# A two-layer block on one core: small fp32 products regrouped, bias rows at the head, two sets of scan tables

## The chip, the cores and the metric

The kernel runs on one core of a Trainium2 chip. The metric is device time in microseconds of one execution, lower is better; the time of a kernel is the median of its runs.

## The reference, cut to what matters

Two layers over 1024 tokens of width 1024, in fp32. The change touches the first layer alone:

```python
h = rmsnorm(x, norm_mix_pre)
q, k, v, u, g_attn, g_ssm = jnp.split(h @ w_in, SPLITS, axis=-1)
y_attn = sliding_window_attention(q, k, v, sinks, rel_bias) @ w_attn_branch
z = gelu(s5_ssm(u, lam_re, lam_im, log_dt, b_re, b_im, c_re, c_im, d_skip))
z = z * sigmoid(z @ w_glu)
merged = sigmoid(g_attn) * y_attn + sigmoid(g_ssm) * (z @ w_ssm_branch)
x = x + rmsnorm(merged @ w_out, norm_mix_post)
```

The attention has 8 query heads of 64 over 2 key heads; a block of 128 queries sees its own and the previous block of keys, with a bias by bucketed distance and a sink per head. The scan has 32 groups of 16 channels, each with a complex diagonal state of 64. A feed-forward block follows, and then the second layer with three gated branches.

## The kernel before, in words

Large products are done in f16 with each operand split into a high and a low half (`split`, L134, one ACT and one DVE operation): three f16 products of 128x128 by 512 for one in fp32. Most go by Strassen's scheme: `strassen` (L267) registers a unit that runs `pair_products` (L189) for a pair of 128-column blocks, seven products of 12 matmuls into four PSUM banks, and a preparation, `prep` (L151), that loads the weights through SP into one of four `raw` buffers and makes seven pairs of halves. `linear2` (L333) is the plain form with 512 rows of weights.

Units stand in `units` in the order of the text and are emitted so, each unit's preparation two units ahead (L1484). The order of instructions on each engine isn't the text's: the framework's planner issues, by its own estimate of times, the earliest operation in the text that is ready. So products of different units are mixed on PE, and each engine then runs its list strictly in order. An operation on a piece of memory waits for all earlier ones in the text that touch the same bytes. Most memory is one array, the arena, addressed in KB by hand (`A32(kb, n)`), so two uses of the same KB order each other. PSUM has two tags of four banks, `bank` for the f16 products and `aux` for the rest.

The units that matter, in the order of the text:

- The head (L526): eight tiles of x are loaded, normalized (ACT squares, POOL power, DVE scaling), turned on PE and split.
- `first_pair` (L359) for keys and values and for half of the queries, then key copies and `sums_later` (L498), then `strassen` for the other half of the queries.
- The bias (L571): eight products spread one head's row of 384 over 128 partitions, ACT copies them, a POOL DMA stores 1.5 MB, and a second one reads it back along diagonals into `bias_t`.
- The scan's parameters (L623): some hundred small DVE operations in a chain (exponentials, sine and cosine, powers), with loads through POOL; scratch comes from `tmp` at 92 to 108 KB. They leave `Ar`, `Ai`, `Bf`, `CT`, `Fs` and others.
- Attention (L810), block by block: `attend(n)` (L760) makes logits of 8 heads into aux banks, DVE adds the bias and takes the row maximum (L773), ACT does the exponentials, DVE scales (L786) into one of two buffers `Pb` at 92 to 108 KB. `values(n - 1)` (L788) turns the probabilities four tiles at a time, ACT copies them (L802), and products of 256 columns go into 64 of the 128 partitions of a bank (L805).
- Two Strassen units for u, whose results are stored through `us` at 132 to 140 KB to DRAM, then four for the attention's gates (`gate_ahead(GA)`).
- The scan (L978): for each of four chunks `ssm_tables(uc)` makes Ft, CA and Gt on DVE, the products `pwk` (L919) of the table Kt (copied to `Wsb`, then eight POOL DMAs) and turned Gt; `ssm_scan(uc)` (L935) makes S (L942), rotates, scans and rotates back on DVE, and then the output products `py` (L967 with Kt, L969 with CA and the states) and a gelu. The arena of the scan starts at 56 KB, where the queries lie.
- Four gates for the scan's branch, four `linear2` with `w_attn_branch`, the GLU (L1006 to L1021) that reads z back, and the branch with `w_ssm_branch`.

Products between fp32 operands show as two records (two weight loads and two matmuls) in the profile, transposes as one. A product over 64 partitions, or into 64, uses half of the array: `64*128` in a row is 64 input rows by 128 output columns, `128*64` the other way.

## Time and profile before

| | us |
|---|---|
| median of 3 runs | 2021.39 |
| lowest and highest run | 2015.39, 2022.36 |
| the profiled execution | 2019.8 |
| its span | 2018.1 |
| PE busy | 1972.1 (98%) |
| DVE busy | 1535.8 (76%) |
| ACT busy | 897.6 (44%) |

The span is the profiled execution from its first to its last instruction. A matmul's length in the profile includes its tail, which overlaps the next one; what a product takes in a stream is seen from start to next start. The granted clock (PEclk) is TensorE's, as a share of full speed.

### The profile page before, as it was taken

Reading aid. Unit: us, or ns where it says so; the run is one execution under the profiler, and the core shown is the slowest. Engines: PE = TensorE matmul, PEld = TensorE weight load, DVE = VectorE, ACT = ScalarE, POOL = GpSimd, SP = SyncE. Lnnn points to the kernel's source line nnn. Section 1 sums busy time; section 2 is a strip of 40 time slices with the busy share of each in tenths; the row PEclk is TensorE's granted clock in tenths of the full one; section 3 lists DMA queues with packets and bytes.
Section 4 is the critical chain, followed back from the end, with each engine's and each line's share of the span. In section 5 each row is a group of like instructions: output and inputs, shape, how many; then the busy total and the mean of one; then the engine's idle time right before and its main releaser. Section 6 shows DMA issues by size and latency. Waiting matters only on the chain. (4 is left out here: it accounts for less than half of the span.)

```text
span 2018.1 us, 25890 instructions
## 1 busy us (share of the span) xinstructions
PE 1972.1 (98%) x9536; PEld 939.9 (47%) x9536; DVE 1535.8 (76%) x2830; ACT 897.6 (44%) x1691; POOL 93.1 (5%) x157
## 2 busy tenths in 40 slices
PE   7989999999999999999999998999999999999998
PEld 4434545554454444444445444454444444444443
DVE  7787678777758876877876767679788797889843
ACT  7326553234346634724626645435333343345411
POOL 1000010110010000000000021000000000000000
PEclk9989999899999999999999999999999999999999
DMA  5322072477422122122122422111212133332122
GB/s 178 101 89 74 32 131 70 128 230 266 151 84 73 43 63 63 42 63 63 56 67 94 140 88 80 50 46 50 64 54 72 43 89 78 77 90 80 62 78 85
DMA packets 132880, 176.01 MB, mean 87 GB/s; under 512 B 12281, under 2 KB 98549, under 8 KB 132624
## 3 DMA queue, kind: packets, MB, share of 16 engines
q1 hardware_dynamic: 124736, 160.46, 24.6%
q0 software_dynamic: 5840, 12.84, 3.7%
q8 instruction: 75, 1.23, 0.2%
q10 hardware_dynamic: 2176, 1.05, 0.2%
q14 instruction: 53, 0.43, 0.1%
HBM read 138.01 MB, written 30.93 MB: 84 GB/s over the span
## 5 line engine op out<-in xcount | busy, mean ns | idle before, releaser
L206 PE MATMUL b<-arena,whi 128*128 128x512 f16 x2044 | 776.4, 380 | 6.4 <-DVE u L235 3.0
L207 PE MATMUL b<-arena,whi 128*128 128x512 f16 x2044 | 776.8, 380 | 1.3 <-DVE arena L136 1.3
L208 PE MATMUL b<-arena,wlo 128*128 128x512 f16 x2044 | 776.4, 380 | 0.0
L135 ACT ACTIVATE whi<-raw 128x512 f16<-128x512 f32 x553 | 332.2, 620 | 517.0 <-PE b L207 246.6
L136 DVE SCALAR_TENSOR_TENSOR wlo<-raw,whi 128x512 f16<-128x512 f32 x553 | 369.7, 678 | 77.0 <-ACT whi L135 75.7
L207 PEld LDWEIGHTS <-whi 128*128 128x128 f16 x2044 | 200.2, 98 | 249.5 <-issue 16.4
L206 PEld LDWEIGHTS <-whi 128*128 128x128 f16 x2044 | 200.4, 98 | 242.5 <-issue 6.5
L208 PEld LDWEIGHTS <-wlo 128*128 128x128 f16 x2044 | 200.3, 98 | 242.3 <-issue 6.1
L251 DVE SCALAR_TENSOR_TENSOR c<-b,u 128x512 f32<-128x512 f32 x204 | 139.5, 685 | 54.5 <-PE b L208 54.3
L413 PEld LDWEIGHTS <-arena 128*128 128x128 f16 x1152 | 112.7, 98 | 133.3
L413 PE MATMUL po<-arena 128*128 128x512 f16 x384 | 84.0, 379 | 0.0
L413 PE MATMUL pf<-arena 128*128 128x512 f16 x384 | 84.0, 379 | 0.0
L413 PE MATMUL pw<-arena 128*128 128x512 f16 x384 | 83.0, 379 | 0.0
L352 PE MATMUL pl<-arena,whi 128*128 128x512 f16 x320 | 82.3, 379 | 0.1
L229 DVE SCALAR_TENSOR_TENSOR u<-b,p 128x512 f32<-128x512 f32 x79 | 54.2, 686 | 35.5 <-PE b L208 33.2
L235 DVE SCALAR_TENSOR_TENSOR u<-b,u 128x512 f32<-128x512 f32 x79 | 54.2, 686 | 33.3 <-PE b L208 33.1
L381 PE MATMUL pq<-arena,whi 128*128 128x512 f16 (+1 forms) x288 | 78.3, 357 | 0.0
L224 ACT ACTIVATE p<-b 128x512 f32<-128x512 f32 x79 | 46.2, 585 | 46.9 <-PE b L208 46.8
L432 ACT ACTIVATE hn<-xr 128x512 f32<-128x512 f32 x32 | 19.9, 623 | 90.5 <-issue 40.1
L841 ACT ACTIVATE c<-c 128x512 f32<-128x512 f32 x60 | 37.6, 628 | 41.7 <-DVE c L251 41.7
L135 ACT ACTIVATE arena<-c 128x512 f16<-128x512 f32 x67 | 41.9, 626 | 24.0 <-DVE c L1370 20.6
L1097 ACT ACTIVATE c<-c 128x512 f32<-128x512 f32 x45 | 28.3, 630 | 53.1 <-DVE c L251 53.0
(325 smaller groups left out, 2157.1 us busy)
## 6 DMA issues: line engine op xcount, KB each, us to landing
raw<-in_w_in_dram SPq DMA_DIRECT2D x86, 512.0 KB, 4.0
raw<-in_w_ff_in_dram SPq DMA_DIRECT2D x32, 512.0 KB, 4.5
raw<-in_w_ff_out_dram SPq DMA_DIRECT2D x32, 512.0 KB, 3.7
fetch<-gdr SPq DMA_DIRECT2D x32, 256.0 KB, 4.8
xr<-xdr SPq DMA_DIRECT2D x32, 256.0 KB, 3.5
gdr<-c SPq DMA_DIRECT2D x24, 256.0 KB, 2.0
arena<-in_x_dram SPq DMA_DIRECT2D x8, 512.0 KB, 10.1
raw<-in_w_out_dram SPq DMA_DIRECT2D x8, 512.0 KB, 5.1
```

Source lines behind the costliest of these rows:

```text
L135: ACT(hi, src, AF.Copy, scale=scale)
L136: STT(lo, src, scale, hi, ALU.mult, ALU.subtract)
L206: MM(b[:, 0:n], whi[:, k], act[0][:, i, k, sl], start=(first and k == 0), stop=False, skip_group_check=not first)
L207: MM(b[:, 0:n], whi[:, k], act[1][:, i, k, sl], start=False, stop=False, skip_group_check=not first)
L208: MM(b[:, 0:n], wlo[:, k], act[0][:, i, k, sl], start=False, stop=(k == nk - 1), skip_group_check=not first)
L224: ACT(v["p1"], o1, AF.Copy, scale=scale)
L229: STT(v["u2"], o2, scale, v["p1"], ALU.mult, ALU.add)
L235: STT(v["u3"], o, scale, v["u2"], ALU.mult, ALU.add)
L251: STT(d, vw(o), scale, vw(v[u]), ALU.mult, ALU.add)
L352: MM(bs[s], w[:, k], a[:, k, s * H:(s + 1) * H], start=(k == 0 and w is hi and a is act[0]), stop=(k == 3 and w is lo))
L381: MM(o, w[:, k % 4], a, start=(k == 0 and w is hi and a is ahi), stop=(k == 7 and w is lo))
L413: MM(bs[s], part(a), w[:, s * H:(s + 1) * H], start=(k == 0 and a is ahi and w is whi), stop=(k == nk - 1 and a is alo))
```

## The change

- **Bias.** One product makes all eight rows on 8 partitions, at the head, right after the second tile of x is issued. A small DRAM buffer takes them, and a DMA spreads them to 128 copies in DRAM; both are on SP. The read along diagonals moves from POOL to SP and stands right after the first two projections.
- **Values.** The transposes are grouped by key half and key head, and one bank takes all products of a block, 512 columns each, into the lower 64 partitions for key head 0 and the upper for 1, in turn. This permutes the rows of the branch's input, so `linear2` can load its weights in that order (`by_kv`), by two DMAs of 64 partitions.
- **Parameters' scratch** moves from 92 to 108 KB to 131 to 136 KB, and some of it to 142 to 144 KB.
- **pwk** goes to four column groups (partitions 0, 32, 64 and 96), and is copied by eight small ACT copies a chunk.
- **py** is a function of its own, `ssm_out`: first all products with Kt, then those with CA, the two row halves in turn.
- **Two sets** of Kt, Ft and CA; the tables of chunk uc + 1 stand in the text between scan and output products of chunk uc. Vt gets a place of its own.

```diff
@@ -330,12 +330,20 @@
         return add
-    def linear2(W, c0, act, cb, scale, early=None):
+    def linear2(W, c0, act, cb, scale, early=None, by_kv=False):
         ws = []
         def prepare():
-            raw = load_k(W, lambda w: w.rearrange("(k p) n -> p k n", p=P), c0)
+            if by_kv:
+                raw = pw.tile([P, 4, 256], F32, tag="raw", name=nm("raw"), bufs=NR)
+                for a in range(2):
+                    nc.sync.dma_start(out=raw[64 * a:64 * a + 64],
+                                      in_=W[256 * a:256 * a + 256].rearrange("(k p) n -> p k n", p=64)[:, :, c0:c0 + 256])
+            else:
+                raw = load_k(W, lambda w: w.rearrange("(k p) n -> p k n", p=P), c0)
             for c in range(2):
                 ws.append(hl_tile())
...
@@ -522,6 +530,29 @@
     a21_1 = Flat(144)
     g_pre = A32(140, D)
     K32 = [A32(92 + 8 * q, 4 * H).rearrange("p (k t) -> p k t", k=4) for q in range(4)]
+    bias_t = A32(84, 8 * 256).rearrange("p (h s) -> p h s", h=8)
+    sink = small([P, 8], "sink")
+    bdr = pdr.tile([P, 8 * 384], F32, tag="bdr", name="bdr")
+    def bias_rows():
+        relb = small([33, 8], "relb")
+        nc.vector.memset(relb, 1.0)
+        nc.gpsimd.dma_start(out=relb[0:32, :], in_=I["rel_bias"])
+        hot, row = A32(88, 384)[0:33, :], A32(89.5, 384)[0:8, :]
+        nc.gpsimd.dma_start(out=hot, in_=I["onehot"])
+        pb = aux("pbias")
+        MM(pb[0:8, 0:384], relb, hot, start=True, stop=True)
+        nc.scalar.copy(row, pb[0:8, 0:384])
+        bds = pdr.tile([1, 8 * 384], F32, tag="bds", name="bds")
+        nc.sync.dma_start(out=bds[0].rearrange("(h i) -> h i", h=8), in_=row)
+        nc.sync.dma_start(out=bdr, in_=bds[0].partition_broadcast(P))
+        nc.gpsimd.dma_start(out=sink, in_=I["sinks"][0].partition_broadcast(P))
+    def bias_read():
+        skew = bass.AP(bdr.tensor, bdr.offset + 127, [[8 * 384 - 1, P], [384, 8], [1, 256]])
+        nc.sync.dma_start(out=bias_t, in_=skew)
     @do
...
                 nc.sync.dma_start(out=g_pre, in_=I["norm_mix_pre"][0].partition_broadcast(P))
             if t == 1:
+                bias_rows()
                 prepare(1)
         for t in range(NT):
             h = A32(124 + 4 * (t % 3), D)
...
     @do
     def _():
+        bias_read()
...
         sums_later(hC, K32)
     strassen(w_in, 256, hC, nothing, UNH * 0.125, dest=lambda c, s, sl: q_t[:, 2 + c, s * H:(s + 1) * H])
-    @do
-    def _():
-        relb = small([33, 8], "relb")
-        nc.vector.memset(relb, 1.0)
-        nc.gpsimd.dma_start(out=relb[0:32, :], in_=I["rel_bias"])
-        hot = A32(92, 384)[0:33, :]
-        nc.gpsimd.dma_start(out=hot, in_=I["onehot"])
-        relrep = A32(94, 8 * P)[0:33, :].rearrange("p (h m) -> p h m", h=8)
-        nc.vector.tensor_copy(relrep, relb.unsqueeze(2).to_broadcast([33, 8, P]))
-        vrow = A32(108, 8 * 384).rearrange("p (h i) -> p h i", h=8)
-        for h in range(8):
-            pb = aux("pbias")
-            MM(pb[:, 0:384], relrep[:, h, :], hot, start=True, stop=True)
-            nc.scalar.copy(vrow[:, h, :], pb[:, 0:384])
-        bdr = pdr.tile([P, 8 * 384], F32, tag="bdr", name="bdr")
-        nc.gpsimd.dma_start(out=bdr, in_=vrow.rearrange("p h i -> p (h i)"))
...
@@ -601,12 +610,14 @@
     dsk = A32(140, G * C)[0:C, :].rearrange("p (r a c) -> p r a c", r=NP, a=2)
     Fs = A32(150, 512).rearrange("p (i r n) -> p i r n", i=2, r=NP)
     mags = small([P, 2, 16], "mags")
-    toff = [92.0]
-    def tmp(n):
+    toff = [131.0]
+    def tmp(n, kb=None):
+        if kb is not None:
+            return A32(kb, n)
         a = A32(toff[0], n)
         toff[0] += n * 4 / KB
-        assert toff[0] <= 108
+        assert toff[0] <= 136
         return a
...
@@ -631,12 +642,12 @@
         plp = aux("plp")
         for i in range(3):
             nc.tensor.transpose(plp[:, i * 16:(i + 1) * 16], L16[:, i, :], ident[0:16, 0:16])
-        prm = tmp(48).rearrange("p (i r) -> p i r", i=3)
...
         TT(t1, nr, li, ALU.mult)
         TT(f_i, f_i, t1, ALU.subtract)
         TT(f_i, f_i, den, ALU.mult)
-        braw = tmp(512).rearrange("p (i r c) -> p i r c", i=2, r=NP)
+        braw = tmp(512, 142).rearrange("p (i r c) -> p i r c", i=2, r=NP)
...
-        tb1 = tmp(256).rearrange("p (r c) -> p r c", r=NP)
-        tb2 = tmp(256).rearrange("p (r c) -> p r c", r=NP)
+        tb1 = tmp(256, 131).rearrange("p (r c) -> p r c", r=NP)
+        tb2 = tmp(256, 132).rearrange("p (r c) -> p r c", r=NP)
         cmul(Bf[:, 0], Bf[:, 1], frb, fib, braw[:, 0], braw[:, 1], tb1, tb2)
         for i, n_ in enumerate(("c_re", "c_im")):
-            craw = tmp(256).rearrange("p (u q) -> p u q", u=4)
+            craw = tmp(256, 133 + i).rearrange("p (u q) -> p u q", u=4)
             nc.gpsimd.dma_start(out=craw, in_=I[n_][0].rearrange("(u g) c p -> (g c) u p", u=4))
             pc_ = aux("pc")
...
@@ -786,26 +801,22 @@
             TS(pr[:, h, s0:], pr[:, h, s0:], s8[:, h:h + 1], None, ALU.mult)
     def values(n):
         pr = Pb[n % 2]
-        for kv in range(2):
-            pv = aux("pvo")
-            for par in range(2):
-                pt = aux("pt")
-                for i in range(2):
-                    h = kv * 4 + par + 2 * i
-                    for half in range(2):
-                        if n or half:
-                            nc.tensor.transpose(pt[:, (half * 2 + i) * P:(half * 2 + i + 1) * P],
-                                                pr[:, h, half * P:(half + 1) * P], ident)
-                b0 = 0 if n else 256
-                pts = A32(142 + 2 * (2 * kv + par), H)
-                nc.scalar.copy(pts[:, b0:], pt[:, b0:])
-                for half in range(2):
-                    if n or half:
-                        MM(pv[par * 64:(par + 1) * 64, 0:256], vtok[:, n - 1 + half, kv * 64:(kv + 1) * 64],
-                           pts[:, half * 256:half * 256 + 256], start=(half == 0 or n == 0), stop=(half == 1))
-            sl = (slice(None), slice(2 * kv, 2 * kv + 2), slice(n * P, (n + 1) * P))
-            split(at[0][sl], at[1][sl], pv[:, 0:256].rearrange("p (c q) -> p c q", c=2), SA)
+        parts = [(half, kv) for half in range(0 if n else 1, 2) for kv in range(2)]
+        pts = {}
+        for half, kv in parts:
+            pt = aux("pt")
+            for i in range(4):
+                nc.tensor.transpose(pt[:, i * P:(i + 1) * P], pr[:, 4 * kv + i, half * P:(half + 1) * P], ident)
+            pts[half, kv] = A32(142 + 2 * (2 * half + kv), H)
+            nc.scalar.copy(pts[half, kv], pt)
+        pv = aux("pvo")
+        for half, kv in reversed(parts):
+            MM(pv[kv * 64:(kv + 1) * 64, :], vtok[:, n - 1 + half, kv * 64:(kv + 1) * 64], pts[half, kv],
+               start=(half == 1), stop=(half == parts[0][0]))
+        sl = (slice(None), slice(None), slice(n * P, (n + 1) * P))
+        split(at[0][sl], at[1][sl], v4(pv), SA)
     @do
...
         return a
     Ut = xa(4096).rearrange("p (g n) -> p g n", g=G)
-    Kt = xa(1024).rearrange("p (g m) -> p g m", g=8)
-    Ft = xa(1024).rearrange("p (i r n) -> p i r n", i=2, r=4)
-    CA = xa(2 * 4 * 9 * 16).rearrange("p (i r d c) -> p i r d c", i=2, r=4, d=9)
+    Kts = [a.rearrange("p (g m) -> p g m", g=8) for a in (xa(1024), A32(136, 1024))]
+    Fts = [a.rearrange("p (i r n) -> p i r n", i=2, r=4) for a in (xa(1024), A32(142, 1024))]
+    CAs = [a.rearrange("p (i r d c) -> p i r d c", i=2, r=4, d=9) for a in (xa(2 * 4 * 9 * 16), A32(131, 2 * 4 * 9 * 16))]
     Gt = xa(1024).rearrange("p (i r d c) -> p i r d c", i=2, r=4, d=8)
-    Vt = Gt.rearrange("p i r d c -> p i r (d c)")
+    Vt = A32(146, 1024).rearrange("p (i r n) -> p i r n", i=2, r=4)
     GT = xa(1024).rearrange("p (i r m) -> p i r m", i=2, r=4)
     Wsb = xa(1024)[0:C, :].rearrange("p (r a m) -> p r a m", r=4, a=2)
     r8t = xa(512).rearrange("p (r n) -> p r n", r=4)
...
             rows = slice(a * 64, (a + 1) * 64)
+            for i in range(2):
+                for r in range(4):
+                    MM(pk[32 * r:32 * r + C, 0:P], Bf[rows, i, p0 + r, :],
+                       CA[rows, i, r, 0:8, :].rearrange("p d c -> p (d c)"), start=(i == 0), stop=(i == 1))
             for r in range(4):
-                for i in range(2):
-                    MM(pk[0:C, r * P:(r + 1) * P], Bf[rows, i, p0 + r, :],
-                       CA[rows, i, r, 0:8, :].rearrange("p d c -> p (d c)"), start=(i == 0), stop=(i == 1))
-            nc.scalar.copy(Wsb[:, :, a, :], pk[0:C, :].rearrange("p (r m) -> p r m", r=4))
+                nc.scalar.copy(Wsb[:, r, a, :], pk[32 * r:32 * r + C, 0:P])
         TT(Wsb[:, :, :, 0:C], Wsb[:, :, :, 0:C], dsk[:, p0:p0 + 4], ALU.add)
         for j in range(8):
...
+        Ft = Fts[uc % 2]
         S = [aux("S") for _ in range(2)]
         for i in range(2):
...
              Ft[:, 0, :, 0:P - 1], Ft[:, 1, :, 0:P - 1], ta, tb)
+    def ssm_out(uc):
+        U = Ut[:, 8 * uc:8 * uc + 8, :]
+        Kt, CA = Kts[uc % 2], CAs[uc % 2]
         pys = [aux("py") for _ in range(2)]
+        cols_ = [slice(r * P, (r + 1) * P) for r in range(4)]
+        for r in range(4):
+            for a in range(2):
+                MM(pys[a][:, cols_[r]], Kt[:, 2 * r + a, :], U[:, 2 * r + a, :], start=(r == 0), stop=False,
+                   skip_group_check=(r > 0))
+        for r in range(4):
+            for i in range(2):
+                for a in range(2):
+                    rows = slice(a * 64, (a + 1) * 64)
+                    MM(pys[a][:, cols_[r]], CA[rows, i, r, 1:9, :].rearrange("p d c -> p (d c)"), Ht[rows, i, r, :],
+                       start=False, stop=(i == 1), skip_group_check=(r > 0))
         for a in range(2):
-            rows = slice(a * 64, (a + 1) * 64)
-            for r in range(4):
-                g = 2 * r + a
-                o = pys[a][:, r * P:(r + 1) * P]
-                MM(o, Kt[:, g, :], U[:, g, :], start=True, stop=False)
-                for i in range(2):
-                    MM(o, CA[rows, i, r, 1:9, :].rearrange("p d c -> p (d c)"), Ht[rows, i, r, :],
-                       start=False, stop=(i == 1))
             ACT(U.rearrange("p (r a) n -> p a r n", a=2)[:, a], pys[a].rearrange("p (r n) -> p r n", r=4),
                 AF.Gelu_apprx_tanh)
         if uc % 2:
...
     @do
     def _():
-        nc.vector.memset(Kt, 0.0)
+        for Kt in Kts:
+            nc.vector.memset(Kt, 0.0)
         uv = udr.rearrange("(g c) (j n) -> j c g n", c=C, j=8)
         for j in range(8):
             nc.gpsimd.dma_start(out=Ut[(7 - j) * C:(8 - j) * C], in_=uv[j])
+        ssm_tables(0)
         for uc in range(4):
-            ssm_tables(uc)
             ssm_scan(uc)
+            if uc < 3:
+                ssm_tables(uc + 1)
+            ssm_out(uc)
     for c0 in range(0, 8, 2):
...
-        linear2(I["w_attn_branch"][0], c0 * P, at, cb_attn, 1.0, lambda c0=c0: fetch_gates(GA, c0))
+        linear2(I["w_attn_branch"][0], c0 * P, at, cb_attn, 1.0, lambda c0=c0: fetch_gates(GA, c0), by_kv=True)
     zf = A32(56, 4 * T).rearrange("p (c j n) -> p c j n", c=4, j=8)
```

## Rows read from the trace of the kernel before

**Rows 1.** The page, part 1: busy time and share of the span, instructions.

```profile
PE 1972.1 (98%) x9536; PEld 939.9 (47%) x9536; DVE 1535.8 (76%) x2830; ACT 897.6 (44%) x1691; POOL 93.1 (5%) x157
```

**Rows 2.** Busy time by stretch: start:end length, PE, PEld, DVE, ACT, POOL, PEclk, DMA share, GB/s.

```profile
87.00:474.00 387.00, 377.68 (x1910) 193.16 (x1909) 289.80 (x763) 160.34 (x354) 30.95 (x54) 0.97 0.42 119
263.00:444.00 181.00, 179.69 (x1016) 99.89 (x1015) 148.88 (x286) 65.41 (x108) 18.87 (x36) 0.97 0.50 134
```

**Rows 3.** The same view, three stretches with a low granted clock.

```profile
91.60:95.00 3.40, 3.40 (x9) 0.92 (x8) 0.21 (x1) 0.88 (x2) 1.59 (x3) 0.50 0.28 111
...
142.00:150.00 8.00, 8.00 (x23) 2.70 (x24) 5.41 (x27) 0.00 (x0) 0.00 (x0) 0.52 0.19 75
361.30:371.50 10.20, 10.20 (x34) 6.40 (x34) 5.21 (x14) 1.77 (x3) 2.21 (x4) 0.50 0.36 94
```

**Rows 4.** Waits: PE's over the span, then one of DVE's; total us, times, longest.

```profile
PE tr L446 <- DVE arena L539: 14.5, 4, 8.0
PE lg L771 <- DVE m L773: 7.0, 2, 4.6
...
DVE arena L614 <- DMA arena<-in_b_im_dram: 3.6, 1, 3.6
```

**Rows 5.** Timeline of PE at 87 us: start, length, engine, line, operation, count.

```profile
86.70 5.80 PE L584 MATMUL pbias<-arena 33*128 33x384 f32 x16
```

**Rows 6.** DMA issues by name: count, size of one, median time to landing.

```profile
raw<-in_w_attn_branch_dram SPq DMA_DIRECT2D x4, 512.0 KB, 4.1
```

**Rows 7.** Timeline of PE within one attention block; the last row is the next block's.

```profile
185.62 1.08 PE L805 MATMUL pvo<-arena 128*64 128x256 f32 x4
186.63 0.66 PE L798 MATMUL pt<-ident,arena 128*128 128x128 f32 x4
187.22 0.70 PE L771 MATMUL lg<-arena 64*128 64x256 f32 x4
...
202.21 0.70 PE L771 MATMUL lg<-arena 64*128 64x256 f32 x4
```

**Rows 8.** Timeline of PE: column halves in turn, full-width products; weight loads of the first (groups by line).

```profile
308.26 1.97 PE L942 MATMUL S<-arena 128*64 128x128 f32 x32
...
1699.01 3.60 PE L1429 MATMUL pp<-arena 128*128 128x512 f32 x8
...
L942 PEld LDWEIGHTS S<-arena 128*64 128x64 f32 x128 | 6.9, 137 | 1.4 <-issue 0.8 <-ACT whi L135 0.4 <-ACT arena L933 0.2
```

**Rows 9.** Timeline of PE: the pwk products of chunk 0, one py round of chunk 1.

```profile
294.13 3.24 PE L919 MATMUL pwk<-arena 64*16 64x128 f32 x32
...
358.89 0.49 PE L967 MATMUL py<-arena 128*128 128x128 f32 x2
359.31 0.71 PE L969 MATMUL py<-arena 64*128 64x128 f32 x4
359.95 0.49 PE L967 MATMUL py<-arena 128*128 128x128 f32 x2
```

**Rows 10.** Timeline of ACT: a copy out of PSUM, and a small operation.

```profile
194.33 0.59 ACT L802 COPY arena<-pt 128x512 f32<-128x512 f32 x1 [2.26 <-PE pt L798]
194.82 0.21 ACT L779 ACTIVATE es<-es 128x8 f32<-128x8 f32 x1
```

**Rows 11.** Groups by line and shape, PE: count, busy us, mean ns, idle before.

```profile
L969 PE MATMUL py<-arena 64*128 64x128 f32 x128 | 25.1, 324 | 0.6 <-DVE arena L621 0.5
...
L967 PE MATMUL py<-arena 128*128 128x128 f32 x64 | 16.2, 337 | 0.0
```

**Rows 12.** Timeline of DVE before the GLU, then L352 alone by stretch (columns of rows 2).

```profile
467.95 3.83 DVE L136 SCALAR_TENSOR_TENSOR arena<-arena 128x1024 f16<-128x1024 f32 x2 [2.98 <-ACT arena L135]
...
443.60:473.60 30.00, 29.94 (x139) 13.60 (x140) 1.00 0.84 276
420.00:443.60 23.60, 11.82 (x54) 5.29 (x54) 1.00 0.80 259
```

**Rows 13.** Timeline of DVE: the probabilities of one block scaled.

```profile
199.60 2.18 DVE L786 TENSOR_SCALAR arena<-arena,s 128x256 f32<-128x256 f32 x8
```

More of the change, by code (lines that the diff above doesn't have):

```diff
@@ L555 @@
     first_pair(w_in, 0, hC, a21_1, cb_q0, UNH * 0.125)
-    bias_t = A32(84, 8 * 256).rearrange("p (h s) -> p h s", h=8)
-    sink = small([P, 8], "sink")
     @do
     def _():
+        bias_read()
         nc.vector.tensor_copy(kk[0:64, 1, :], kk[64:128, 0, :])
@@ L569 @@
     strassen(w_in, 256, hC, nothing, UNH * 0.125, dest=lambda c, s, sl: q_t[:, 2 + c, s * H:(s + 1) * H])
-    @do
-    def _():
-        relb = small([33, 8], "relb")
-        nc.vector.memset(relb, 1.0)
-        nc.gpsimd.dma_start(out=relb[0:32, :], in_=I["rel_bias"])
-        hot = A32(92, 384)[0:33, :]
-        nc.gpsimd.dma_start(out=hot, in_=I["onehot"])
-        relrep = A32(94, 8 * P)[0:33, :].rearrange("p (h m) -> p h m", h=8)
-        nc.vector.tensor_copy(relrep, relb.unsqueeze(2).to_broadcast([33, 8, P]))
-        vrow = A32(108, 8 * 384).rearrange("p (h i) -> p h i", h=8)
-        for h in range(8):
-            pb = aux("pbias")
-            MM(pb[:, 0:384], relrep[:, h, :], hot, start=True, stop=True)
-            nc.scalar.copy(vrow[:, h, :], pb[:, 0:384])
-        bdr = pdr.tile([P, 8 * 384], F32, tag="bdr", name="bdr")
-        nc.gpsimd.dma_start(out=bdr, in_=vrow.rearrange("p h i -> p (h i)"))
-        skew = bass.AP(bdr.tensor, bdr.offset + 127, [[8 * 384 - 1, P], [384, 8], [1, 256]])
-        nc.gpsimd.dma_start(out=bias_t, in_=skew)
-        nc.gpsimd.dma_start(out=sink, in_=I["sinks"][0].partition_broadcast(P))
     G, PS_, C = 32, 64, 16
@@ L624, in _ @@
     def _():
-        L16 = tmp(3 * P)[0:16, :].rearrange("p (i m) -> p i m", i=3)
+        L16 = tmp(3 * P, 142)[0:16, :].rearrange("p (i m) -> p i m", i=3)
         nc.gpsimd.dma_start(out=L16[:, 0, :], in_=I["lam_re"][0].rearrange("(r a) p -> r (a p)", a=2))
@@ L633, in _ @@
             nc.tensor.transpose(plp[:, i * 16:(i + 1) * 16], L16[:, i, :], ident[0:16, 0:16])
-        prm = tmp(48).rearrange("p (i r) -> p i r", i=3)
+        prm = tmp(48, 143.5).rearrange("p (i r) -> p i r", i=3)
         nc.vector.tensor_copy(prm, plp[:, 0:48].rearrange("p (i r) -> p i r", i=3))
@@ L638, in EXP @@
         def EXP(dst, src, n):
-            save = toff[0]
+            save, toff[0] = toff[0], 131.0
             xc, t, k, r, p = (tmp(n) for _ in range(5))
@@ L655, in SINCOS @@
         def SINCOS(sn, cs, y, n):
-            save = toff[0]
+            save, toff[0] = toff[0], 131.0
             t, q, r, r2, p, s, c, o = (tmp(n) for _ in range(8))
@@ L690, in SINCOS @@
             toff[0] = save
+        toff[0] = 135.0
         dt_ = small([P, 16], "dt")
@@ L706, in _ @@
         TT(Ai[:, 1, :], mags[:, 0, :], snd[:, 0, :], ALU.mult)
+        toff[0] = 131.0
         for m in (1, 2, 4):
@@ L711, in _ @@
                  Ar[:, m:m + 1, :].to_broadcast([P, m, 16]), Ai[:, m:m + 1, :].to_broadcast([P, m, 16]), t1, t2)
-        nr, den, f_r, f_i, t1 = (tmp(16) for _ in range(5))
+        toff[0] = 135.75
+        nr, den, f_r, f_i = (tmp(16) for _ in range(4))
+        t1 = tmp(16, 131)
         TS(nr, Ar[:, 1, :], -1.0, None, ALU.add)
@@ L891, in ssm_tables @@
         p0 = 4 * uc
+        Kt, Ft, CA = Kts[uc % 2], Fts[uc % 2], CAs[uc % 2]
         nc.vector.tensor_copy(Ft[:, :, :, 0:16], Fs[:, :, p0:p0 + 4, :])
```

## The prediction

> **What bounds the kernel now.** I read the page first. TensorE (PE) is busy for 98% of the span [rows 1], and a busy PE is not yet PE at its peak, so the question is what its time is spent on. The stretch that the change touches comes next: from 87 to 474 us PE idles only 9.3 of 387 us (387.0 less 377.7), while DVE is busy for 289.8 us; from 263 to 444 us, where the scan chunks run, PE idles 1.3 us [rows 2]. Work taken off PE there moves the end, if something else is ready to fill its place; earlier tables as such can't win more there than those 1.3 us and the clock. The clock is the third view: in three stretches the granted clock is 0.50 to 0.52, about 1.2 of 2.4 GHz, and each follows small products or an idle stretch of PE [rows 3]. The waits are the fourth: 7.0 us of PE's idle time are the attention logits waiting for DVE's row maxima, and DVE itself stood 3.6 us before a load of b_im, with those maxima queued behind [rows 4].
>
> **The change, part by part.** The sum is made against the profiled execution's own 2019.8 us, which is 1.6 us under the median of the runs shown (2021.39), so I make no correction.
>
> *Bias.* Sixteen PE records of 384 columns in 5.8 us [rows 5] become one product of 8 rows, two records. Two such records are 0.7 us, with the change of shapes 0.9. They now lie at the head, where PE waits 14.5 us for the first normalized rows [rows 4], but I count them: 4.9 us saved. The low clock at 91.6 us follows these products; 3.4 us at half speed cost 1.7 us [rows 3]. The head gets three things in exchange. On POOL the one-hot load stands among the powers of the norm. On SP two stores (the rows, then 1.5 MB of copies, waiting for the first to land) stand before raw weight loads. ACT gets one small copy. I take nothing: x is issued earlier on SP and the diagonal read is wanted only some 75 us later. If that cover fails, the head is later by 0 to 3 us. Below nothing isn't possible, since the head loses no work. The branch weights come in eight issues of half the partitions instead of four that land in 4.1 us [rows 6]. They are issued ahead of use into four buffers, so nothing; uncovered, up to 4 x 4.1 us.
>
> *Start of the attention.* The parameters' scratch lay at 92 to 108 KB, where the probabilities are written, so the first block had to wait for the last complex product of the parameters, and that for b_im. The scratch now lies elsewhere, and the parameters can begin while the first projections run. I count the 7.0 us of waiting [rows 4] and the low clock after it (8 us at 0.52, 3.8 us [rows 3]) as gone. Against that, the scratch at 131 to 136 KB lies on the buffer of the u projections, whose results now wait for the parameters; and b_re and b_im still load late, behind the last readers of the parameters' columns. Both go into the losses below.
>
> *Values.* For a block now: four groups of four transposes, 0.59 us each from start to next start, and four groups of four product records, 1.01 us each, together 6.4 us [rows 7]. After: sixteen transposes in one group, 0.59 + 12 x 0.109 = 1.9 us (0.109 is the step inside a group: 0.66 less the last one's 0.33, by three). Then eight records of 512 columns, alternating between the two column halves. Do halves run beside each other? The scan's S products have that pattern: 32 records of 128 columns in 1.97 us, 0.06 each [rows 8], where records one after another take 0.10 (the pwk group, 32 in 3.24 us [rows 9]). So a pair costs one record's 0.43 us (eight full-width ones take 3.60 us with the last one's tail [rows 8]), four pairs with the change of shapes 2.0 us. A block saves 6.4 - 1.9 - 2.0 = 2.5 us, seven of them 17.5; block 0, with half the keys, 1.3. Together 18.8 us; if halves don't overlap, about 5.
>
> *pwk.* The same 32 records over four column groups: at S's pace 1.97 instead of 3.24 us, 1.27 a chunk, 5.1 us in four. Bounds: 0, if 16-column groups don't overlap, and 8.4 if four run at once (a quarter of 3.24 and the change of shapes, 1.1 us a chunk). I take S, the nearest row. ACT makes eight copies of 16x128 instead of two of 16x512: between 0.2 and 0.6 us each [rows 10], 0.4 to 3.6 us a chunk, off PE's path since the products that need them now come a chunk later.
>
> *py.* Now the order for each group pair is two records of the full array, then four over 64 rows, 1.06 us a round [rows 9]; 48 records are eight rounds, 8.5 us, and the counts confirm four chunks [rows 11]. After: 16 full records at 0.109 and one start, 2.0 us, then 32 alternating between row halves at S's pace, 1.9 us. That saves 4.6 us a chunk, 18.5 in all (from 11, if row halves don't overlap either).
>
> *Second set of tables.* No PE work goes. One more memset on DVE; nothing for PE except the clock: the low stretch at 361 us lies on py products and what follows; with these dense, I count its 5.1 us (10.2 x 0.5, [rows 3]) as gone.
>
> Sum: 4.9 + 1.7 + 7.0 + 3.8 + 18.8 + 5.1 + 18.5 + 5.1 = 64.9 us.
>
> **What is late next.** DVE's work hardly shrinks: 289.8 of 387 us now, of 322 then, 90%; and 148.9 in a stretch of 181 that should lose 18.5 + 5.1 + 5.1 = 28.7, or 98% [rows 2]. Other projections can be moved about, but not without waits. I take 12 us lost, some 4 tenths of those 28.7, between 0 and all of it. So 2019.8 - 64.9 + 12 = **1967 us**.
>
> The Trainium skill, TensorE: Matmul & The Clock Gate, section The mechanism, says that a weight load overlaps a running matmul only where the row groups differ. The halves of values and pwk share their rows, so by that their loads (137 ns for S's [rows 8]) would lie open and the two savings shrink to those of the second rival. The S records, whose halves share rows too, go against it: at 0.06 us each there is no room for 137 ns.
>
> **Rivals.**
>
> *DVE or the scan becomes the bound.* The second input of the GLU is ready at 471.8 us (467.95 + 3.83, [rows 12]), and PE comes to it at about 473.5 (the attention branch has 4 x 48 records, 54 of them before 443.6 us and 138 after it at 0.216 [rows 12]): 1.7 us to spare. If DVE can't go faster than now from 263 to 444 us, the 28.7 us aren't got there; half of the 12 us of losses is then in them. 2019.8 - 64.9 + 28.7 + 6 = 1990 us. For it: 98%. Against: chunks no longer wait for each other's tables, and the attention starts earlier.
>
> *Halves stay one after another.* Values save 5 instead of 18.8, pwk nothing: 1967 + 13.8 + 5.1 = 1986 us. Groups broken up by other products would cost alike: the order on PE is a planner's, not the text's. Against it: the S row.
>
> *The attention block becomes serial.* Four transposed tiles take all four aux banks. Then logits of the next block can't start before values are done. From logits to scaled probabilities is 14.6 us now (187.22 [rows 7] to 201.78 [rows 13]); transposes 1.9, last copy 0.6, products 2.0 and split 1.3 make 20.4, and a copy queued behind the next block's exponentials (some 4 us) 24.4, against a period of 15.0 (187.22 to 202.21, [rows 7]). Eight blocks are then 75 us later. The chain to the GLU gains about 42 us from the earlier start (142 [rows 3] to about 100, my estimate: the queries are ready at about 87 us, and the parameters get what DVE has free from 30 us on) and 24 from shorter products; from 23.4 us a block on, PE waits for it. At 24.4 the wait is 8 us, with a slow restart 13: 2033 us, slower than before. Against it: the planner frees a bank with each copy.
>
> **How the numbers follow.** Forecast 0.62, with its own range 1952 to 1980; DVE or scan 0.24 (1980 to 2012); halves 0.10; serial block 0.04. A measurement of this kernel tells about 0.5%, 10 us, from no change. The low end is no loss and pwk by fours: 2019.8 - 64.9 - 3.3 = 1951.6, so 1950. The high end is the first rival with 3 us at the head and part of the clock not given back, 1996. Faster: all of the forecast and the halves and most of the first rival, 0.91; same 0.05, from the far end of that rival; slower 0.04.
>
> **What would show it.** Right: eight pvo records a block in about 2 us; 48 py records in about 4 us; no pbias group near 87 us; attention in full step before 110 us; no low clock at 91, 142 and 361 us. Wrong: PE idle before the first GLU products, or records of two halves starting a full record apart; a low clock elsewhere; logits starting only after the block's last values; a first transpose later than now.

## The result and the profile after

Measured beside it, the kernel before had a median of 2021.88 us; the changed kernel's is 1988.85 us (1986.79 to 1990.61 over four runs). The ratio is 0.9836, with a 95% interval of 0.9803 to 0.9870: 33 us faster, inside the whole range (1950 to 1996) and 22 us above the figure forecast. It is outside the forecast's own range (1952 to 1980), in that of the first rival (1980 to 2012), and within 1.2 us of that rival's 1990. Whether that rival's mechanism was at work is the first question of the experiments.

The page of the changed kernel, part 1 (busy time, share of the span, instructions; [rows 1] before):

```profile
PE 1925.0 (97%) x9462; PEld 910.4 (46%) x9462; DVE 1534.0 (77%) x2822; ACT 895.2 (45%) x1698; POOL 91.1 (5%) x155
```

TensorE lost 47.1 us of busy time, DVE 1.8. The span fell only by 30.1 us, from 2018.1 to 1988.0, so TensorE idles some 17 us more. All of it lies before the mixer's output products `po`: their first starts at 536.0 us before and at 505.7 us after, and from there to the end both take 1482 us. So the account is made from 0 to that start. Its view is busy time by stretch: start:end length, PE, PEld, DVE, ACT, POOL, granted clock, DMA share, GB/s. The stretches are those before `po`, two like [rows 2], and the two longest at low clock, like [rows 3]:

```profile
0.00:505.70 505.70, 464.65 (x2518) 233.59 (x2519) 411.20 (x943) 239.24 (x495) 39.05 (x73) 0.98 0.48 142
...
87.00:506.00 419.00, 392.88 (x2135) 192.20 (x2134) 343.97 (x837) 185.26 (x405) 30.02 (x52) 0.97 0.47 139
222.00:423.00 201.00, 184.43 (x1174) 93.83 (x1170) 166.12 (x304) 77.12 (x143) 18.88 (x36) 0.97 0.52 151
131.25:141.50 10.25, 8.56 (x21) 3.40 (x21) 8.74 (x39) 5.80 (x21) 0.00 (x0) 0.50 0.14 53
411.15:421.40 10.25, 5.97 (x17) 2.17 (x18) 8.36 (x13) 0.33 (x1) 0.00 (x0) 0.50 0.37 126
```

Before, TensorE was busy 511.9 of the 536.0 us; it now is for 464.65 of 505.7. Where the clock is at 0.50, I count half of the busy time as the clock's. This is an estimate: in the kernel before, dense f16 products follow each other at 0.216 us at a clock of 1.00 and at 0.43 at 0.50 (371.60 and 368.69 us), but a py round takes 1.06 and 1.87 us, so for small products half is a little too much. Before, 21.5 us of busy time lie in such stretches, after, 17.9. Without that half (10.7 and 9.0 us) the work is 501.1 and 455.7 us, 45.4 us less, where the four product terms of the sum make 47.3 (4.9 + 18.8 + 5.1 + 18.5). So work gives 45.4 us, the clock 1.7, and idle time takes back 16.9 (from 24.1 to 41.0 us). Of the low stretches, those at 91 and 361 us are gone, the one at 139 us came to 131 us, and new ones stand at 411 and 445 us (3.4 us): 23.9 us in all both times.

Where TensorE waited from 85 us to `po` in the changed kernel (in all, times, longest; [rows 4] before):

```profile
PE py L990 <- DVE arena L626: 7.3, 1, 7.3
PE pwk L932 <- DVE arena L626: 5.2, 3, 2.1
PE pl L360 <- ACT arena L135: 2.3, 1, 2.3
PE lg L786 <- DVE m L788: 2.0, 6, 1.1
PE pc L754 <- DMA arena<-in_c_re_dram: 1.4, 1, 1.4
PE S L957 <- ACT arena L947: 1.4, 1, 1.4
PE b L206 <- DVE u L229: 1.4, 1, 1.4
```

The logits' 7.0 us became 2.0. In their place stand other waits, of which the longest is one for the last chunk's output products.

The small products themselves, by name (duration least, median, most; first and last start), one attention block and one chunk, beside [rows 7 to 9]:

```profile
L816 PE MATMUL pvo<-arena x8: 592/592/643, 165.6 to 166.9; 128*64 128x512 f32 x8
...
L932 PE MATMUL pwk<-arena x32: 269/269/280, 273.4 to 273.8; 64*16 64x128 f32 x32
...
L990 PE MATMUL py<-arena x32: 272/272/373, 317.5 to 319.2; 64*128 64x128 f32 x32
L984 PE MATMUL py<-arena x16: 275/275/288, 315.6 to 317.3; 128*128 128x128 f32 x16
```

Eight values products end within 2 us of the first start, 48 py products take 3.6 us between first and last start, and 32 pwk products start within 0.4 us and end within 0.7, where they took 3.24.

### The profile page after: what moved, and what is told of

Same layout as the page of the kernel before. It is cut to its first block, busy times and chain, and to the rows that moved or that the text cites. A ratio compares the mean times of both kernels' runs of the same rounds, so it can differ in the third digit from the quotient of the medians.

```text
span 1988.0 us, 25746 instructions
## 1 busy us (share of the span) xinstructions
PE 1925.0 (97%) x9462; PEld 910.4 (46%) x9462; DVE 1534.0 (77%) x2822; ACT 895.2 (45%) x1698; POOL 91.1 (5%) x155
## 5 line engine op out<-in xcount | busy, mean ns | idle before, releaser
L136 DVE SCALAR_TENSOR_TENSOR wlo<-raw,whi 128x512 f16<-128x512 f32 x553 | 369.5, 678 | 76.9 <-ACT whi L135 76.1
L207 PEld LDWEIGHTS <-whi 128*128 128x128 f16 x2044 | 200.1, 98 | 250.7 <-issue 15.6
L360 PE MATMUL pl<-arena,whi 128*128 128x512 f16 x320 | 86.7, 390 | 2.4 <-ACT arena L135 2.3
```

Of the source, the lines that this page charges most:

```text
L136: STT(lo, src, scale, hi, ALU.mult, ALU.subtract)
L207: MM(b[:, 0:n], whi[:, k], act[1][:, i, k, sl], start=False, stop=False, skip_group_check=not first)
L360: MM(bs[s], w[:, k], a[:, k, s * H:(s + 1) * H], start=(k == 0 and w is hi and a is act[0]), stop=(k == 3 and w is lo))
```

## The experiments

Each was measured in turn with the kernel before, and the intervals of the ratios are 0.2 to 0.3% (4 to 6 us) to each side. Differences from the changed kernel's 1988.85 us are differences of medians taken at different times, between which the kernel before moved by up to 3.8 us (2021.88 to 2025.68). So 3 to 5 us are near what can be told apart; they are read together with the spans of the profiles, which show the same signs. "Work" is TensorE's busy time up to `po`, less half of what of it lies in stretches at 0.50. The nine runs that have the same products show 451.1 to 455.7 us of it, 453.8 in the mean, and the changed kernel's 455.7 is the highest. So differences under some 5 us say nothing.

| run | median us | ratio (95%) | against changed, us | span us | `po` at us |
|---|---|---|---|---|---|
| e1_swap | 1980.67 | 0.9787 (0.9760 to 0.9813) | -8.2 | 1980.4 | 497.6 |
| e2_head | 1985.81 | 0.9816 (0.9790 to 0.9842) | -3.0 | 1982.4 | 500.2 |
| e3_oneset | 1984.15 | 0.9804 (0.9778 to 0.9830) | -4.7 | 1981.8 | 499.1 |
| e4_values | 2002.73 | 0.9901 (0.9876 to 0.9925) | +13.9 | 2000.5 | 518.8 |
| e5_params | 1984.90 | 0.9811 (0.9791 to 0.9831) | -4.0 | 1984.0 | 501.6 |
| e6_py | 2003.44 | 0.9903 (0.9882 to 0.9923) | +14.6 | 2003.7 | 520.4 |
| e7_pwk | 1992.93 | 0.9854 (0.9834 to 0.9874) | +4.1 | 1991.9 | 509.7 |
| e8_best | 1981.20 | 0.9793 (0.9772 to 0.9813) | -7.7 | 1977.8 | 495.2 |
| e9_both | 1977.97 | 0.9779 (0.9749 to 0.9810) | -10.9 | 1976.2 | 493.5 |
| e10_scratch | 1984.45 | 0.9813 (0.9783 to 0.9844) | -4.4 | 1984.2 | 501.5 |
| e11_bias | 1995.79 | 0.9874 (0.9842 to 0.9905) | +6.9 | 1992.9 | 510.2 |
| e12_late | 2002.11 | 0.9901 (0.9873 to 0.9929) | +13.3 | 2001.2 | 517.6 |

**The wait before the last py products.** First what DVE does in the changed kernel at 399 us, in the scan of the last chunk, then ACT and TensorE (timeline: start, length, engine, line, operation; idle time before it and its releaser):

```profile
399.63 0.69 DVE L964 TENSOR_TENSOR arena<-arena 128x512 f32<-128x512 f32 x1
405.20 1.94 DVE L136 SCALAR_TENSOR_TENSOR arena<-arena 128x1024 f16<-128x1024 f32 x1 [4.88 <-ACT arena L135]
407.06 0.68 DVE L965 TENSOR_TENSOR arena<-S,arena 128x512 f32<-128x512 f32 x1
...
409.97 1.90 DVE L136 SCALAR_TENSOR_TENSOR arena<-arena 128x1024 f16<-128x1024 f32 x1
411.79 1.21 DVE L970 TENSOR_TENSOR_SCAN arena<-arena 128x512 f32<-128x512 f32 x1
...
403.20 3.84 ACT L135 ACTIVATE arena<-arena 128x1024 f16<-128x1024 f32 x2 [5.12 <-DMA arena<-zdr]
...
407.71 0.38 PE L360 MATMUL pl<-arena,wlo 128*128 128x512 f16 x1
415.43 0.80 PE L990 MATMUL py<-arena 64*128 64x128 f32 x4 [7.34 <-DVE arena L626]
```

Two splits of the GLU's input (L136 on 128x1024) stand in the middle of the scan (L964, L965, ..., L970). The first waits 4.88 us for ACT, which waits for a load that was issued at 395.65 us; the scan's own operations, which need nothing of it, stand behind. TensorE has branch products left, but they stand behind py in its own list. The splits write 72 to 88 KB, where the first set of tables lies. With one set they had to wait for the last chunk's products; the last chunk now uses the other set, so the first is free early, and the planner puts the splits there. The test lets the chunks take the sets the other way round:

```diff
-        Kt, Ft, CA = Kts[uc % 2], Fts[uc % 2], CAs[uc % 2]
+        Kt, Ft, CA = Kts[(uc + 1) % 2], Fts[(uc + 1) % 2], CAs[(uc + 1) % 2]
```

(and the same in the scan and in the output.)

> The two sets of tables change places, so that the last chunk uses the set at 72 KB and the GLU's input can't be split there before that chunk's output products. Theory A (places in the lists): DVE's stand of 4.9 us in the last scan goes, TensorE's wait of 7.3 us before the last py products falls under 2 us, the low clock at 411 us (5.1 us lost) goes too: 1978 to 1982 us. Theory B (DVE or the chain to the GLU is the bound, my first rival): the splits only move behind the last products, the GLU's first tanh (450.4 us in the changed kernel) comes at most 4 us earlier: 1985 to 1990 us.

Measured: 1980.67 us. Its timeline of DVE and TensorE at the same place:

```profile
398.56 0.69 DVE L964 TENSOR_TENSOR arena<-arena 128x512 f32<-128x512 f32 x1
399.28 0.69 DVE L965 TENSOR_TENSOR arena<-S,arena 128x512 f32<-128x512 f32 x1
...
411.82 1.93 DVE L136 SCALAR_TENSOR_TENSOR arena<-arena 128x1024 f16<-128x1024 f32 x1
...
405.51 0.49 PE L990 MATMUL py<-arena 64*128 64x128 f32 x4 [0.87 <-DVE arena L626]
```

And the busy time from 400 to 425 us, in the changed kernel and then with the sets swapped:

```profile
400.00:425.00 25.00, 17.66 (x99) 9.21 (x97) 18.12 (x24) 9.02 (x9) 0.35 (x1) 0.80 0.56 205
```

```profile
400.00:425.00 25.00, 24.13 (x142) 12.65 (x140) 20.34 (x26) 11.06 (x13) 2.22 (x4) 1.00 0.91 292
```

The stall, the wait and the low clock at 411 us are gone; the first tanh of the GLU comes at 439.9 instead of 450.4 us. A low stretch of 6.8 us at 434 us takes a part back. DVE did the same work, so DVE's load wasn't the bound: the cause was the splits' place in its list.

**The head.** In the changed kernel TensorE's list begins with the bias product; in the second timeline (DVE) the first normalization L571 stands behind two weight splits:

```profile
8.56 1.44 PE L545 MATMUL pbias<-arena,relb 33*8 33x384 f32 x2 [8.56 <-DMA relb<-in_rel_bias_dram]
12.93 1.33 PE L454 MATMUL tr<-ident,arena 128*128 128x128 f32 x5 [2.93 <-DVE arena L571]
...
10.38 1.29 DVE L136 SCALAR_TENSOR_TENSOR wlo<-raw,whi 128x512 f16<-128x512 f32 x2 [4.66 <-ACT whi L135]
11.59 1.28 DVE L571 SCALAR_TENSOR_TENSOR arena<-arena,rs 128x1024 f32<-128x1024 f32 x1
```

```diff
             if t == 1:
-                bias_rows()
+                bias = bias_rows()
                 prepare(1)
...
             put_T(halves(h), t, hC, a21_1, lambda q, t: K32[q][:, :, (t % 4) * P:(t % 4 + 1) * P], later=True)
+        bias_product(*bias)
```

Here `bias_rows` ends with the loads, and `bias_product` holds the product, the copy and the stores.

> The bias product, its copy and the two stores stand behind the loop over x's blocks instead of ahead of it; the loads stay where they are. Theory A (the wait of 8.6 us for the table's load at the head of TensorE's list is what makes the head late): first transposes at 8 instead of 12.9 us, third projection pair at 68.5 instead of 71.6 us, time 3 us less than the changed kernel's 1989.7, so 1985 to 1988 us. Rival: ACT's and DVE's order in the head sets it, not TensorE's wait: first transposes still after 11 us, time 1989 to 1991 us.

Measured: 1985.81 us, and the first transposes of this kernel are back:

```profile
8.17 1.97 PE L454 MATMUL tr<-ident,arena 128*128 128x128 f32 x8 [8.17 <-DVE arena L574]
```

3.0 us less by the medians, as theory A had it, but the head itself gives only part of it: the third projection pair starts at 69.8 us, where 68.5 was expected, against 71.6 in the changed kernel and 68.5 before. So 1.9 of the 3.1 us that the head had lost are back. The spans of the two profiles differ by 5.6 us; half of its busy time at low clock is 5.6 us where the changed kernel has 9.0.

**One set of tables.** `Kts`, `Fts` and `CAs` hold one set twice, `Vt` lies on `Gt` again, and the loop is

```diff
-        ssm_tables(0)
         for uc in range(4):
+            ssm_tables(uc)
             ssm_scan(uc)
-            if uc < 3:
-                ssm_tables(uc + 1)
             ssm_out(uc)
```

> One set of tables, the scan's work area on the G matrices again, and the order of the kernel before (tables, scan, output of a chunk, then the next); all else as changed. Theory A (the second set brings nothing by itself, the dense products do): 1984 to 1994 us, scan chunks 5 to 6 us shorter than the 40.5 of before each. Theory B (the chunks need the second set to get shorter, chain of tables, scan and products bounds): a chunk's pitch stays at 38 us or more, the last py ends after 435 us, 1996 to 2005 us.

Measured: 1984.15 us, 4.7 us under the changed kernel. The last py of the four chunks start at 293.4, 329.6, 364.7 and 400.0 us, 35.5 us apart (38.0 before, where I had taken 40.5), where two sets have 319.2, 358.9, 396.7 and 423.0. So the dense products shorten the chunks without a second set, and with the tables ahead the first outputs only come later. Against e1_swap (two sets, without the stall), which was measured at the same time, one set is 3.5 us slower by the medians, and no run of the one reaches into the other's (1978.62 to 1982.11 and 1983.50 to 1984.49); by the spans it is 1.4 us. So the second set as such is no loss, and at most a small gain.

**The three groups of products, one undone at a time.** e4_values has the values loop and the branch loads of before; e6_py and e7_pwk have the product loops of before:

```diff
-        for r in range(4):
-            for a in range(2):
-                MM(pys[a][:, cols_[r]], Kt[:, 2 * r + a, :], U[:, 2 * r + a, :], start=(r == 0), stop=False,
-                   skip_group_check=(r > 0))
...
+        for a in range(2):
+            for r in range(4):
+                MM(o, Kt[:, g, :], U[:, g, :], start=True, stop=False)
+                for i in range(2):
+                    MM(o, CA[rows, i, r, 1:9, :].rearrange("p d c -> p (d c)"), Ht[rows, i, r, :],
+                       start=False, stop=(i == 1))
```

> The values products and the branch weights as before, all else as changed. Theory A (TensorE's work is the bound, what is taken from it reaches the end): the forecast's 18.8 us come back, 2004 to 2012 us. Theory B (DVE or the chain to the GLU is the bound): the extra products fill the 26 us in which TensorE idles between 87 and 506 us, 1989 to 1999 us.

> The output products of a chunk in the order of before (full array, then two over a row half, group by group), all else as changed. Theory A (what TensorE is spared reaches the end): the forecast's 18.5 us come back, 2004 to 2010 us. Theory B (the scan's chain on DVE bounds, products fill waits): at most the 7.3 us of wait and 5.1 us of clock before the last chunk are lost to be filled, 1990 to 1998 us.

> The pwk products and their copies as before, all else as changed. By the changed kernel's pace (32 records within about 0.5 us where they took 3.24) TensorE gets 2.7 us a chunk back, 10.9 in all: 1998 to 2001 us if that reaches the end. By the pace of S, which the forecast took, 5.1 us: 1993 to 1996 us. Rival (pwk waits for DVE anyway, 5.2 us in three times, so its length is hidden in part): 1988 to 1992 us.

Measured: 2002.73, 2003.44 and 1992.93 us. Work up to `po`: 471.3, 472.5 and 463.1 us against 455.7 in the changed kernel, 15.6, 16.8 and 7.4 us more (each 1.9 us more against the mean of 453.8). The times give back 13.9, 14.6 and 4.1. The first two lie about 1 us below theory A's bands and 4 to 5 us above theory B's. pwk's work lies between the two paces offered, its time between the bands of the second pace and of the rival, less than 1 us from each, so a part of it is hidden, as the rival had it: with the slow products TensorE's waits before them are 3.5 instead of 5.2 us, and up to `po` it idles 36.9 instead of 41.0 us.

**The start of the attention.** The parameters of the scan in the changed kernel: their first products by name, then POOL's loads (timeline):

```profile
L644 PE MATMUL plp<-ident,arena x3: 207/208/229, 89.8 to 90.0; 16*128 16x16 f32 x3
...
90.42 1.21 POOL L743 DMA_DIRECT2D arena<-in_b_re_dram  x1 [52.78 <-PE plp L644]
115.86 0.78 POOL L751 DMA_DIRECT2D arena<-in_c_im_dram  x1 [24.23 <-DVE arena L699]
116.62 0.75 POOL L751 DMA_DIRECT2D arena<-in_c_re_dram  x1
```

The columns of the parameters had been loaded 50 us before, but the three transposes stand behind the third projection pair in TensorE's list. The loads of c, whose place now lies on scratch that DVE uses first, stand behind DVE's work there; in the kernel before they were issued at 67.7 us. The logits stand behind the transposes of c (`pc`) in TensorE's list in both kernels (timeline before, then changed):

```profile
96.56 1.06 PE L739 MATMUL pc<-ident,arena 128*64 128x128 f32 x8
97.55 0.48 PE L771 MATMUL lg<-arena 64*128 64x128 f32 x2
```

```profile
120.57 1.06 PE L754 MATMUL pc<-ident,arena 128*64 128x128 f32 x8 [1.39 <-DMA arena<-in_c_re_dram]
121.56 0.49 PE L786 MATMUL lg<-arena 64*128 64x128 f32 x4
```

So the first logits start 24 us later than before, not earlier. Three runs bear on this.

e10_scratch gives the parameters the scratch of before (92 to 108 KB) and leaves the rest:

```diff
-    toff = [131.0]
+    toff = [92.0]
...
-            craw = tmp(256, 133 + i).rearrange("p (u q) -> p u q", u=4)
+            craw = tmp(256).rearrange("p (u q) -> p u q", u=4)
```

> The parameters' scratch at 92 to 108 KB as before, all else as changed. Theory A (my forecast's term: the move saves the wait of 7.0 us at the attention's start and 3.8 us of clock): 1996 to 2000 us. Theory B (the parameters did not come earlier, so the move only changed what waits for them): 1986 to 1992 us, first logits again near 98 us with a wait behind them.

Measured: 1984.45 us, 4.4 us under the changed kernel and below theory B's band too. The logits by name, and two of TensorE's waits in this run:

```profile
L780 PE MATMUL lg<-arena x128: 272/376/792, 90.3 to 217.7; 64*128 64x256 f32 x112, 64*128 64x128 f32 x16
...
PE py L984 <- DVE arena L624: 6.8, 1, 6.8
PE lg L780 <- DVE m L782: 6.0, 5, 2.8
```

The logits start at 90.3 us, 31 us earlier than with the new scratch, and wait 6.0 us in all, as in the kernel before. The move was to save this wait; it does, and saves nothing by it.

e5_params puts the parameters' block ahead of the third pair and loads b and c to 136 to 140 KB.

> The parameters' block stands ahead of the third projection pair in the program, and b and c are loaded to 136 to 140 KB, which is free early; all else as changed. Theory A (the parameters came late because their three transposes stood behind the third pair in TensorE's list, at 89.8 us, and c_re's load behind DVE's scratch): transposes before 70 us, first logits by 95 instead of 121.6 us, no low clock at 131 us (5.1 us), no wait for c_re (1.4 us): 1982 to 1985 us. Rival (DVE, busy 28.8 of the 30 us from 90 on, is the limit, so the waits come back elsewhere): logits earlier, but 1988 to 1991 us.

Measured: 1984.90 us, inside theory A's range, but by half of its steps only. The transposes run at 71.2 us and the first logits at 98.1, both a little later than expected, and no low stretch is left at 131 us; in exchange one of 6.8 us begins at 79.1 us, within this wait:

```profile
PE pc L753 <- DMA arena<-in_c_im_dram: 4.4, 1, 4.4
```

e12_late goes the other way: e9_both (below) with the whole block behind the attention.

> e9_both with the whole block of the parameters behind the attention in the program, its loads at places that are free early. Theory A (nothing of it is wanted before the scan's tables, and ahead of the attention it costs the wait for c_re, the logits' waits and the low clock at 131 us): first logits at 88 to 92 us, no low clock at 131 us, 5 to 8 us under e9_both. Rival (the two u pairs filled TensorE's time while DVE made the parameters; behind the attention they fill less, and the waits come back there): within 3 us of e9_both.

Measured: 2002.11 us, 24.1 over e9_both: both sides missed. The logits start at 88.1 us as expected, and the attention ends 46 us earlier (last values 174.2 us). But the two u pairs, which filled TensorE's time while DVE made the parameters, now have to wait for them, since their results lie on the scratch. The wait, and the stretch in which it falls:

```profile
PE b L206 <- DVE arena L802: 18.8, 1, 18.8
```

```profile
182.50:203.00 20.50, 4.04 (x10) 1.49 (x11) 15.34 (x85) 0.62 (x1) 2.34 (x2) 0.50 0.16 39
```

**The bias rows.** e11_bias makes them as before, behind the third pair.

> The bias rows made by eight products after the third projection pair as before, all else as changed. My forecast's terms (4.9 us of TensorE's work, 1.7 us of clock) less the loss at the head that e2_head showed (3 us): 1991 to 1994 us, first transposes at 8 us again. Rival (the head's loss is as large as the gain): 1987 to 1990 us.

Measured: 1995.79 us, 6.9 over the changed kernel, just above the forecast's band; the first transposes are at 8.0 us. The low stretch at 91.7 us is back, with another at 122.4.

**Together.** e8_best is e3_oneset, e2_head and e5_params in one kernel; e9_both is e1_swap and e2_head.

> One set of tables as in e3_oneset, the bias product behind the first loop as in e2_head, and the parameters ahead as in e5_params, together. Theory A (each takes away a place in a list, and they lie apart): 6 us of e3, 5 of e2 and 5 of the clock at 131 us, 1971 to 1976 us. Rival (a wait that goes at one place comes back at another): 1978 to 1983 us.

> The sets swapped as in e1_swap and the bias product behind the first loop as in e2_head, together. Theory A (two places in the lists that lie far apart, so the gains add): 8.2 and 3.0 us from the changed kernel's 1988.85: 1976 to 1979 us. Rival (in e8_best three such steps did not add): 1980 to 1982 us.

Measured: 1981.20 and 1977.97 us. e8_best lies in the rival's band: the gains (4.7, 3.0 and 4.0 alone) don't add up, and the wait for c_im before its transposes is 6.9 us there. In e9_both they do: 8.2 and 3.0 were expected, 10.9 measured. It has the lowest median of this study, 0.9779 of the time before.

## Why the prediction was right and where it wasn't

**TensorE's work: right in sum, one size clearly off.** Four terms of 47.3 us, measured 45.4. Undone one at a time, the groups put back 15.6 us of work for values (forecast 18.8), 16.8 for py (18.5), 7.4 for pwk (5.1) and 2.1 for the bias (4.9; e11_bias has 457.8 us of work). All four differ from the forecast by less than the spread of the work, and against the mean of the runs alike each is 1.9 us more. The groups in the trace say more: eight values products take 1.9 us to the next product's start (forecast 2.0), the 48 of py 3.9 (3.9), and the 32 of pwk end within 0.7 (1.97). So pwk was sized too small: in the chunk shown 2.6 us are gone where I forecast 1.27, and even the bound that I kept, "four at once", was too low. (Its 8.4 us is 8.6 by my own 1.1 us a chunk.)

Halves that run beside each other were the condition of all this, and the second rival fell with it. So did the rule of the Trainium skill that I set against it (TensorE: Matmul & The Clock Gate, The mechanism), for these shapes: eight values products whose halves share their rows, with their loads, begin and end within 2 us. Another page of the Trainium skill, which I had not weighed, bears it out: TensorEngine Tiling (Array Packing), Key Properties, has different tiles load weights and multiply in parallel. The trace agrees, with 32 pwk products that start within 0.4 us.

**That work reaches the end: right in the main.** Values and py undone came back by 13.9 and 14.6 us, most of their work; of pwk's 7.4 us only 4.1 did. The premise that TensorE's work bounds the stretch, read from [rows 2], holds for the most part.

**The start of the attention, 7.0 + 3.8 us: wrong.** The step "the parameters can begin while the first projections run" failed. They could by their data, but the list on TensorE put their transposes behind the third pair, and the move put the loads of c behind DVE's scratch and the logits behind those. The sign "attention in full step before 110 us" didn't come: its first logits start at 121.6 us. The move of the scratch saved none of the 10.8 us; undone, the kernel is 4.4 us faster (e10_scratch), which is near what can be told apart. The wait of the logits was no price by itself: while they wait, or while the parameters are made, what counts is whether TensorE has other products ahead in its list. That part is argued from e12_late, which took them away and lost 24 us.

**The clock, 10.6 us in three terms: wrong, 1.7 came.** The low stretches at 91 and 361 us did vanish, as the terms said, and that at 142 us only moved. I counted them as gone and no new one; two came, one behind the py wait (gone in e1_swap), one behind the 2.3 us wait for the GLU's input.

**The second set and the tables ahead: sized at nothing, a loss.** I noted one more memset. The cost was a place in memory: the set left free early let the splits of the GLU's input into the last scan. e1_swap shows 8.2 us for that. e3_oneset shows 4.7 for the whole part, so apart from the stall two sets lose nothing.

**The head: at the far end of its bounds.** I took nothing of 0 to 3 us; in the trace the third projection pair starts 3.1 us later than before (71.6 and 68.5), of which e2_head gives 1.9 back. I had looked at POOL's and SP's lists and not at the first entry of TensorE's.

**The 12 us of losses.** With them and the 7.0 us gained, idle time should have grown by 5 us; it grew by 16.9. These 11.9 us, 8.9 of the clock (10.6 less 1.7) and 1.9 of the work make 22.7, and the profiled execution's 1989.7 us is 22.7 over the forecast.

**The first rival gave the figure, not the reason.** Its 1990 us rests on DVE, or the chain to the GLU, being unable to go faster. e9_both has the same DVE work (411.5 us up to `po`, against 411.2) and is 10.9 us faster, and products put back returned most of their length. Its sign, TensorE idle before the first GLU products, is there in small: 2.3 us, and 2.6 in e1_swap. The third rival, a serial attention block, didn't show: the attention's last logits start 44 us earlier than before, though the first start 24 us later, and its eight blocks of values products follow each other every 11.5 us (139.9 to 220.7), where the rival had 20 to 24.

What stays open: why the planner puts the pwk products 2 us too early in three chunks (5.2 us of waits, with one set 7.7) was not tried, nor were loads of c that are issued early enough for e5_params. The best kernel is still 11 us above the 1967 forecast; the 10.8 us for the start of the attention, which no run got in full, are of that size, but that they are the reason is not shown.

## What to carry to other kernels

Products saved on the busy engine reached the end for the most part here, and their sum could be worked out from record starts. What a change that moves buffers costs is found in the order of the lists: for each region that becomes free earlier, ask which operation can now be placed there, what it waits for, and what stands behind it on its engine. A buffer that is moved can also carry a load behind other work, as the loads of c were. And a wait that vanished was not worth its length here where the same engine's next wait was already due; the low clock moved with the waits.

## What the runs showed of the hardware that I had not expected

Products of 64 rows and 16 columns, issued round four column groups, start 32 records within 0.4 us and end within 0.7, where 32 in one column group took 3.24. The granted clock fell within a wait rather than after it in two stalls: in e5_params TensorE stood from 76.4 to 80.8 us and the granted clock was 0.50 from 79.1 to 85.9; in the changed kernel it stood from 408.1 to 415.4 and the clock was 0.50 from 411.15 to 421.4. So each wait cost more than its own length, by an estimated half of the part of the low stretch behind it: 2.6 us (5.1 of the 6.8) and 3.0 us (6.0 of the 10.25).
